# A down projection whose residual is added by an accumulating transfer instead of VectorE

## The chip, the core and the metric

The kernel runs on one core of a Trainium2 chip. The metric is the time of one execution on the device in microseconds (us); the time before is the median of three runs. One profiled execution supplies all the views. TensorE appears in them as PE (matmuls) and PEld (weight loads), VectorE as DVE, ScalarE as ACT, GpSimd as POOL, SyncE as SP.

## What is computed

The reference is a decoder layer of 256 tokens by 2048 channels in float32: gated token mixers, cross-attention into 256 memory tokens, a convolutional gated feed-forward block, and a final RMSNorm. The change touches only the end:

```python
def conv_glu_ffn(u, w_up, conv_w, conv_b, w_down):
    gate, up = jnp.split(u @ w_up, 2, axis=-1)
    gate = causal_dwconv(gate, conv_w, conv_b)
    return (jax.nn.gelu(gate, approximate=False) * up) @ w_down
...
    h = h + conv_glu_ffn(u, ffn_w_up[l], ffn_conv_w[l], ffn_conv_b[l], ffn_w_down[l])
return rms_norm(h, final_norm_g)
```

The down projection is (256 x 5632) times (5632 x 2048). To it the residual `h` is added, each row is scaled by the inverse root of its mean square, and each column by `final_norm_g`.

## The kernel before

Every float32 operand is split into a high and a low part (`hi`, `lo`), and a product is three matmuls: high by high, high by low, low by high. A weight tile of 1 MB (128 x 2048) is loaded by SP into `raw` (three buffers), cast to `hi` by ScalarE and subtracted to `lo` by VectorE (L131 and L132, two pieces of 1024 columns). `hi` and `lo` have five buffers each. `weights()` issues the load and the split of the tile two steps ahead.

**The down projection** runs in two halves of 1024 output columns (`for i in range(2)`). Each half has four output blocks `acc[0..3]` of 128 tokens by 512 columns: blocks 0 and 1 are the first 128 tokens (g = 0), blocks 2 and 3 the others (g = 1). A half is a list of 22 steps over pairs of 128-row slabs of the 5632, and `down_steps` writes the order out by hand:

- an *ordinary step* does two slabs by four blocks by three matmuls: 24 matmuls of 512 columns into `acc`;
- a *seven-product step* (seven per half) does a 2x2 block product by Winograd's scheme with seven block products instead of eight: 21 matmuls. Four of the seven products go to banks of their own, `own[0..3]`, three straight into `acc`. Its weight forms need more preparation (`seven_forms`, L165 to L176): ScalarE casts and VectorE subtracts in turn, and VectorE adds three forms in between. The activation forms come from `input_forms` (L964 to L974), called in the first half alone at `j == 3 * s`.

After the last seven-product step of a half, `own[0..3]` are combined into four blocks `c` (a copy by ScalarE, L1036, and four VectorE operations, L1037 to L1040). The residual comes from `rows_d` in DRAM: four loads of 256 KB into `hr` (two buffers, SP, L1044), each followed by a VectorE addition to `c` (L1045). Two ordinary steps follow in each half while this goes on. In the first half, `acc` is then added to `c` (L1050) and squared for the norm (L1052); the result is kept as `first` and multiplied by `final_norm_g` early in the second half (L995).

**The end of the second half.** The last two steps are held together: block after block gets the 12 matmuls of both, so that block 0 is complete first, and block 3 is done as two pieces of 256 columns. Then, in pinned order, for each block: VectorE adds `acc` to `c` (L1065), ScalarE squares with a row sum (L1067), VectorE multiplies by the norm's weights into `two` (L1069). After block 1 (tokens g = 0) and after the last piece (g = 1): the row sums are reduced (L1073), two small ScalarE operations give the scale `r` (L1074, L1075), VectorE scales the 1024 columns kept from the first half (L1078), ScalarE scales 512 columns of `two` (L1081), VectorE the other 512 (L1083), and three transfers write the rows out. The two halves swap their banks, so `own` of the second half are the `proj` banks, and its `acc` are `lev` (blocks 0 and 1) and `misc` (blocks 2 and 3).

Of the kernel before, what the change touches and what calls it, by code (L numbers as in the profile page):

```python
# [9 lines left out]
F32 = mybir.dt.float32  # L10
# [3 lines left out]
AF = mybir.ActivationFunctionType  # L14
ALU = mybir.AluOpType
# [4 lines left out]
P = 128  # L20
# [29 lines left out]
def down_steps(half):  # L50
    rest = list(range(NST, KF // 2))
    if half:
        rest = rest[-4:] + rest[:-4]
    steps = []
    for s, ordinary in enumerate((3, 2, 2, 2, 2, 1, 1) if half else (2, 2, 2, 2, 2, 2, 1)):
        steps += [(False, rest.pop(0)) for _ in range(ordinary)] + [(True, s)]
    return steps + [(False, k) for k in rest]

# [6 lines left out]
def hybrid_trunk(ctx, tc, xT, memT, par, cst, msk, w_k0, w_ka, w_va, w_hg, w_hv, w_ghg, w_bhg, w_dt,  # L65
                 w_m2, w_gm2, w_bm2, w_out, w_q, w_o, w_up, w_dn, fin_g, outT):
    nc = tc.nc
# [264 lines left out]
    rows_d = dp.tile([T, D], F32, name="rows_d")  # L332
# [651 lines left out]
    for i in range(2):  # L984
        steps = down_steps(i)
        acc = [pj.tile([P, 512], F32, name="proj") for _ in range(4)]
        own = [pl.tile([P, 512], F32, name="lev") for _ in range(2)] \
            + [pm_.tile([P, 512], F32, name="misc") for _ in range(2)]
        if i:
            acc, own = own, acc  # L990
        for j, (seven, q) in enumerate(steps):
            if i == 1 and 4 <= j < 8:

                o = first[:, j - 4, :]
                V.tensor_tensor(out=o, in0=o, in1=gr[:, j % 2 * 512:j % 2 * 512 + 512], op=ALU.mult)  # L995
            if j == 10 * i:
                gr = fd.tile([P, 1024], F32, name="gr")
                nc.sync.dma_start(out=gr, in_=fin_g[i:i + 1, :].partition_broadcast(P))
            last = i == 1 and j >= len(steps) - 2
            if i == 0:  # L1000
                for s in range(NST):
                    if j == 3 * s:
                        input_forms(s)
            w = weights()
            if last and j < len(steps) - 1:
                held = w, q
            elif last:


                for b, c0, c1 in ((0, 0, 512), (1, 0, 512), (2, 0, 512), (3, 0, 256), (3, 256, 512)):  # L1010
                    for x, p in (held, (w, q)):
                        for k in range(2):
                            wh, wl = x(2 * k + b % 2, 512)
                            mm_tok(acc[b][:, c0:c1], inputs(2 * p + k, b // 2),
                                   (wh[:, c0:c1], wl[:, c0:c1]), stop=p == q and k == 1 and c1 == 512)
            elif seven:
                y1, x2, x4 = [(xs[:, q, n, 0:P], xs[:, q, n, P:2 * P]) for n in range(3)]
                a11, y3 = inputs(2 * q, 0), inputs(2 * q, 1)
                a12, a22 = inputs(2 * q + 1, 0), inputs(2 * q + 1, 1)
                one = dict(start=q == 0, stop=q == NST - 1)  # L1020
                mm_tok(own[0], a11, w[0], **one)
                mm_tok(acc[1], x4, w[1])
                mm_tok(own[1], y1, w[2], **one)
                mm_tok(own[2], x2, w[3], **one)
                mm_tok(own[3], y3, w[4], **one)
                mm_tok(acc[0], a12, w[5])
                mm_tok(acc[2], a22, w[6])
            else:
                for k in range(2):
                    for b in range(4):  # L1030
                        mm_tok(acc[b], inputs(2 * q + k, b // 2), w(2 * k + b % 2, 512),
                               start=j == 0 and k == 0, stop=j == len(steps) - 1 and k == 1)
            if seven and q == NST - 1:
                c = fd.tile([P, 4, 512], F32, name="c") if i == 0 else \
                    big.tile([P, 4, 512], F32, name="h")
                S.copy(out=c[:, 0, :], in_=own[0])  # L1036
                V.tensor_tensor(out=c[:, 2, :], in0=own[2], in1=c[:, 0, :], op=ALU.subtract)  # L1037
                V.tensor_tensor(out=c[:, 1, :], in0=own[1], in1=c[:, 2, :], op=ALU.add)
                V.tensor_tensor(out=c[:, 2, :], in0=own[3], in1=c[:, 2, :], op=ALU.add)
                V.tensor_tensor(out=c[:, 3, :], in0=own[1], in1=c[:, 2, :], op=ALU.add)  # L1040
                for b in range(4):
                    hr = fd.tile([P, 512], F32, name="hr", bufs=2)
                    o = 1024 * i + b % 2 * 512
                    nc.sync.dma_start(out=hr, in_=rows_d[b // 2 * P:(b // 2 + 1) * P, o:o + 512])  # L1044
                    V.tensor_tensor(out=c[:, b, :], in0=c[:, b, :], in1=hr,  # L1045
                                    op=ALU.subtract if b == 2 else ALU.add)
        if i == 0:
            for b in range(4):
                g, n = b // 2, b % 2
                V.tensor_tensor(out=c[:, b, :], in0=acc[b], in1=c[:, b, :],  # L1050
                                op=ALU.subtract if b == 2 else ALU.add)
                S.activation(out=acc[b], in_=c[:, b, :], func=AF.Square,  # L1052
                             accum_out=ss[:, g, n:n + 1])
            first = c


    def then(ins):
        tc.keep_in_program_order(ins)

    two = wp.tile([P, 4, 512], F32, name="raw", bufs=3)  # L1060
    for b, c0, c1, slot in ((0, 0, 512, 2), (1, 0, 512, 3), (2, 0, 512, 2), (3, 0, 256, 3),
                            (3, 256, 512, 4)):
        g, n = b // 2, b % 2
        o = c[:, b, c0:c1]
        then(V.tensor_tensor(out=o, in0=acc[b][:, c0:c1], in1=o,  # L1065
                             op=ALU.subtract if b == 2 else ALU.add))
        then(S.activation(out=acc[b][:, c0:c1], in_=o, func=AF.Square,  # L1067
                          accum_out=ss[:, g, slot:slot + 1]))
        then(V.tensor_tensor(out=two[:, b, c0:c1], in0=o, in1=gr[:, n * 512 + c0:n * 512 + c1],  # L1069
# [1 line left out]
        if n == 1 and (g == 0 or slot == 4):  # L1071
            r = fd.tile([P, 2], F32, name="r", bufs=2)
            then(V.tensor_reduce(out=r[:, 0:1], in_=ss[:, g, 0:4 + g], axis=AX.X, op=ALU.add))  # L1073
            then(S.activation(out=r[:, 1:2], in_=r[:, 0:1], func=AF.Ln, bias=eps_t, scale=1.0 / D))  # L1074
            then(S.activation(out=r[:, 1:2], in_=r[:, 1:2], func=AF.Exp, scale=-0.5))  # L1075
            s = r[:, 1:2]
            one = first[:, 2 * g:2 * g + 2, :]
            then(V.tensor_scalar(out=one, in0=one, scalar1=s, scalar2=None, op0=ALU.mult))  # L1078
            nc.sync.dma_start(out=rows[:, g, 0:1024].rearrange("p (n c) -> p n c", n=2), in_=one)
            x, y = two[:, 2 * g, :], two[:, 2 * g + 1, :]  # L1080
            then(S.activation(out=x, in_=x, func=AF.Copy, scale=s))  # L1081
            (nc.scalar if g else nc.sync).dma_start(out=rows[:, g, 1024:1536], in_=x)
            then(V.tensor_scalar(out=y, in0=y, scalar1=s, scalar2=None, op0=ALU.mult))  # L1083
            nc.sync.dma_start(out=rows[:, g, 1536:2048], in_=y)


# [111 lines left out]
```

## Time and profile before

| | |
|---|---|
| median of three runs | 2262.02 us (2260.88 to 2262.89) |
| the profiled execution | 2262.1 us, of which the span of instructions is 2260.3 us |
| PE busy | 2244.1 us, 99% of the span |
| VectorE busy | 1640.1 us, 73% |
| ScalarE busy | 1344.4 us, 59% |
| GpSimd busy | 1.3 us |
| mean granted TensorE clock | 0.998 |

A span is the time from the first instruction to the last. A row of the timeline gives an instruction's start, its duration, its engine and line, what it writes and reads, and in brackets the idle time before it and what ended that. Matmuls are pipelined: one takes 0.39 us from start to end, while the next starts about 0.227 us after it.

### The profile page before, as it was taken

Reading aid. Unit: us, or ns where it says so; the run is one execution under the profiler, and the core shown is the slowest. Engines: PE = TensorE matmul, PEld = TensorE weight load, DVE = VectorE, ACT = ScalarE, POOL = GpSimd, SP = SyncE. Lnnn points to the kernel's source line nnn. Section 1 sums busy time; section 2 is a strip of 40 time slices with the busy share of each in tenths; the row PEclk is TensorE's granted clock in tenths of the full one; section 3 lists DMA queues with packets and bytes.
Section 4 is the critical chain, followed back from the end, with each engine's and each line's share of the span. In section 5 each row is a group of like instructions: output and inputs, shape, how many; then the busy total and the mean of one; then the engine's idle time right before and its main releaser. Section 6 shows DMA issues by size and latency. Waiting matters only on the chain.

```text
span 2260.3 us, 33624 instructions
## 1 busy us (share of the span) xinstructions
PE 2244.1 (99%) x13316; PEld 1937.3 (86%) x13316; DVE 1640.1 (73%) x2648; ACT 1344.4 (59%) x2030; POOL 1.3 (0%) x9
## 2 busy tenths in 40 slices
PE   9999999999999999999999999999999999999997
PEld 8888888888888888888888888888888888888886
DVE  7878879796446677754576755676777777788877
ACT  7566767676446778764456655556555555555544
POOL 0000000000000000000000000000000000000000
PEclk9999999999999999999999999999999999999999
DMA  8744454446555555455566545576555555555653
GB/s 304 247 168 173 167 183 168 168 161 216 193 189 193 179 186 195 168 186 187 194 229 214 202 170 180 177 228 211 190 188 190 193 193 186 186 201 190 233 214 131
DMA packets 86685, 436.91 MB, mean 193 GB/s; under 512 B 24544, under 2 KB 29184, under 8 KB 37504
## 3 DMA queue, kind: packets, MB, share of 16 engines
q1 hardware_dynamic: 69600, 432.36, 54.2%
q10 hardware_dynamic: 16928, 2.42, 0.6%
q8 instruction: 104, 1.70, 0.3%
q14 instruction: 53, 0.43, 0.1%
HBM read 428.42 MB, written 8.42 MB: 193 GB/s over the span
## 4 chain that ended last, share of the span: by engine, by line
PE 96%; DVE 2%; ACT 0%; DMA 0%; issue 0%; DVEq 0%; SPq 0%; ACTq 0%
PE proj L82 88%; PE misc L82 5%; PE lev L82 4%; DVE lo L132 1%; DVE e L523 0%; DVE e L536 0%; DMA raw<-in_w_k 0%; DVE lo L166 0%; PE lev L704 0%; PE lev L768 0%; DMA hr<-rows_d 0%; DVE h L1065 0%; ACT hi L131 0%; PE lev L848 0%; DVE h L1045 0%
## 5 line engine op out<-in xcount | busy, mean ns | idle before, releaser
L132 DVE TENSOR_TENSOR lo<-raw,hi 128x1024 fp32r<-128x1024 f32 x738 | 891.4, 1223 | 438.0 <-ACT hi L131 384.9
L131 ACT CAST hi<-raw 128x1024 fp32r<-128x1024 f32 x737 | 768.1, 1048 | 401.5 <-PE proj L82 387.5
L82 PE MATMUL proj<-s,hi 128*128 128x512 f32 x3952 | 935.0, 392 | 0.6 <-ACT hi L361 0.6
L82 PEld LDWEIGHTS proj<-s,hi 128*128 128x128 f32 x3952 | 732.4, 188 | 146.8 <-ACT hi L131 1.0
L82 PE MATMUL proj<-hi,s 128*128 128x512 f32 x1706 | 534.9, 391 | 0.0
L82 PEld LDWEIGHTS proj<-s,lo 128*128 128x128 f32 x3952 | 495.8, 192 | 12.6 <-ACT s L278 0.5
L82 PE MATMUL proj<-s,lo 128*128 128x256 f32 x3952 | 503.6, 284 | 0.0
L82 PEld LDWEIGHTS proj<-hi,s 128*128 128x128 f32 x1706 | 320.2, 188 | 66.4 <-issue 0.3
L82 PE MATMUL proj<-lo,s 128*128 128x512 f32 x853 | 332.5, 390 | 0.0
L82 PEld LDWEIGHTS proj<-lo,s 128*128 128x128 f32 x853 | 160.2, 188 | 32.2
L263 ACT COPY jt<-proj 128x256 f32<-128x256 f32 x199 | 73.6, 370 | 106.7 <-PE proj L82 106.6
L165 ACT CAST hi<-raw 128x1024 fp32r<-128x1024 f32 (+1 forms) x56 | 51.5, 942 | 89.9 <-DVE raw L173 46.2
L166 DVE TENSOR_TENSOR lo<-raw,hi 128x1024 fp32r<-128x1024 f32 (+1 forms) x56 | 59.9, 1090 | 28.4 <-ACT hi L165 28.0
L667 DVE SCALAR_TENSOR_TENSOR sz<-t,par_t,sz 128x255 f32<-128x255 f32 (+2 forms) x96 | 46.1, 480 | 8.1 <-ACT sz L664 6.9
L935 DVE SCALAR_TENSOR_TENSOR gc<-g,par_t,gc 128x255 f32<-128x255 f32 x88 | 42.3, 480 | 2.0 <-ACT gc L933 0.6
L938 ACT ACTIVATE gc<-gc 128x256 f32<-128x256 f32 x44 | 18.4, 418 | 30.5 <-DVE gc L935 30.5
L82 PE MATMUL proj<-hi,ha 128*128 128x512 f32 x104 | 35.7, 390 | 0.0
L939 DVE TENSOR_TENSOR gc<-gc,r_f 128x256 f32<-128x256 f32 x44 | 18.7, 425 | 21.5 <-ACT gc L938 21.5
L523 DVE TENSOR_TENSOR e<-bb 128x256 f32<-128x256 f32 x96 | 33.6, 420 | 0.0
L536 DVE TENSOR_TENSOR e<-e,kq 128x256 f32<-128x256 f32 x96 | 33.5, 419 | 0.0
L82 PE MATMUL lev<-hi,s 128*128 128x512 f32 x92 | 32.6, 390 | 0.0
L527 ACT ACTIVATE e<-e 128x768 f32<-128x768 f32 x32 | 26.2, 842 | 6.7 <-DVE e L523 6.7
(287 smaller groups left out, 1709.8 us busy)
## 6 DMA issues: line engine op xcount, KB each, us to landing
raw<-in_w_up SPq DMA_DIRECT2D x88, 1024.0 KB, 4.8
raw<-in_w_hg SPq DMA_DIRECT2D x48, 1024.0 KB, 4.8
raw<-in_w_m SPq DMA_DIRECT2D x48, 1024.0 KB, 4.7
raw<-in_w_dn SPq DMA_DIRECT2D x44, 1024.0 KB, 4.8
raw<-in_w_hv SPq DMA_DIRECT2D x16, 1024.0 KB, 4.8
raw<-in_w_ghg SPq DMA_DIRECT2D x16, 1024.0 KB, 4.8
raw<-in_w_bhg SPq DMA_DIRECT2D x16, 1024.0 KB, 4.7
raw<-in_w_gm SPq DMA_DIRECT2D x16, 1024.0 KB, 4.8
```

Source lines behind the costliest of these rows:

```text
L82: ins = PE.matmul(*args, **kwargs)
L131: S.copy(out=hi[:, c - a:d - a], in_=raw[:, c:d])
L132: V.tensor_tensor(out=lo[:, c - a:d - a], in0=raw[:, c:d], in1=hi[:, c - a:d - a].bitcast(F32), op=ALU.subtract)
L165: S.copy(out=hi[:, 0:d - c], in_=raw[:, c:d])
L166: V.tensor_tensor(out=lo[:, 0:d - c], in0=raw[:, c:d], in1=hi[:, 0:d - c].bitcast(F32), op=ALU.subtract)
L263: S.copy(out=tmp, in_=ps[:, T:2 * T])
L523: V.tensor_tensor(out=lev[hw].rearrange("p (n c i) -> p n c i", c=2, i=hw), in0=free(bb, 0, [(2 * hw, nb), (T + hw, 2), (1, hw)]), in1=fre ...
L527: S.activation(out=e[j], in_=e[j], func=AF.Exp)
L536: V.tensor_tensor(out=ev, in0=ev, in1=free(kq, 0, [(2 * hw, nb), (T + hw, 2), (1, hw)]), op=ALU.mult)
L667: V.scalar_tensor_tensor(out=o[:, s:T], in0=raw[:, 0:T - s], scalar=pc("m2_cw", 4 * c + 3 - s), in1=o[:, s:T], op0=ALU.mult, op1=ALU.add)
L935: V.scalar_tensor_tensor(out=gc[:, s:T], in0=g[:, 0:T - s], scalar=pc("f_cw", 3 * c + 2 - s), in1=gc[:, s:T], op0=ALU.mult, op1=ALU.add)
L939: V.tensor_tensor(out=gc, in0=gc, in1=r_f, op=ALU.mult)
```

## The change

Four edits, all in the down projection and the final norm:

1. The residual is added to `c` by one transfer per half with `accum_op=ALU.add`, issued from GpSimd's queue: 128 partitions by two groups of tokens by 1024 columns, 1 MB. The four loads `hr` and the four VectorE additions of a half are gone.
2. The combination of `own` gives block 2 with the other sign, so that all blocks can be added to alike: three `tensor_tensor` and one `scalar_tensor_tensor` instead of four `tensor_tensor`.
3. In both halves an ordinary step moves from before the last seven-product steps to behind them, so that three ordinary steps end a half, not two. The forms of the activations are made at `j == 5 * s // 2`.
4. For tokens g = 0 the scaling is shared in another way: ScalarE takes the 1024 columns of the first half, VectorE the 1024 of `two` in one instruction. For g = 1 nothing but the order in the text changes. The transfers to the output stay.

```diff
-    for s, ordinary in enumerate((3, 2, 2, 2, 2, 1, 1) if half else (2, 2, 2, 2, 2, 2, 1)):
+    for s, ordinary in enumerate((3, 2, 2, 1, 2, 1, 1) if half else (2, 2, 2, 2, 1, 2, 1)):
...
-                    if j == 3 * s:
+                    if j == 5 * s // 2:
                         input_forms(s)
...
                 S.copy(out=c[:, 0, :], in_=own[0])
                 V.tensor_tensor(out=c[:, 2, :], in0=own[2], in1=c[:, 0, :], op=ALU.subtract)
                 V.tensor_tensor(out=c[:, 1, :], in0=own[1], in1=c[:, 2, :], op=ALU.add)
-                V.tensor_tensor(out=c[:, 2, :], in0=own[3], in1=c[:, 2, :], op=ALU.add)
-                V.tensor_tensor(out=c[:, 3, :], in0=own[1], in1=c[:, 2, :], op=ALU.add)
-                for b in range(4):
-                    hr = fd.tile([P, 512], F32, name="hr", bufs=2)
-                    o = 1024 * i + b % 2 * 512
-                    nc.sync.dma_start(out=hr, in_=rows_d[b // 2 * P:(b // 2 + 1) * P, o:o + 512])
-                    V.tensor_tensor(out=c[:, b, :], in0=c[:, b, :], in1=hr,
-                                    op=ALU.subtract if b == 2 else ALU.add)
+                V.tensor_tensor(out=c[:, 3, :], in0=own[3], in1=c[:, 1, :], op=ALU.add)
+                V.scalar_tensor_tensor(out=c[:, 2, :], in0=own[3], scalar=-1.0, in1=c[:, 2, :],
+                                       op0=ALU.mult, op1=ALU.subtract)
+                G.dma_start(out=c.rearrange("p (g n) c -> p g (n c)", g=2),
+                            in_=rows_d.rearrange("(g p) c -> p g c", p=P)[:, :, 1024 * i:1024 * i + 1024],
+                            accum_op=ALU.add)
...
-        then(V.tensor_tensor(out=o, in0=acc[b][:, c0:c1], in1=o,
-                             op=ALU.subtract if b == 2 else ALU.add))
+        then(V.tensor_tensor(out=o, in0=acc[b][:, c0:c1], in1=o, op=ALU.add))
...
-            then(V.tensor_scalar(out=one, in0=one, scalar1=s, scalar2=None, op0=ALU.mult))
+            x, y = two[:, 2 * g, :], two[:, 2 * g + 1, :]
+            if g == 0:
+                then(S.activation(out=one, in_=one, func=AF.Copy, scale=s))
+                then(V.tensor_scalar(out=two[:, 0:2, :], in0=two[:, 0:2, :], scalar1=s, scalar2=None,
+                                     op0=ALU.mult))
+            else:
+                then(V.tensor_scalar(out=one, in0=one, scalar1=s, scalar2=None, op0=ALU.mult))
+                then(S.activation(out=x, in_=x, func=AF.Copy, scale=s))
+                then(V.tensor_scalar(out=y, in0=y, scalar1=s, scalar2=None, op0=ALU.mult))
             nc.sync.dma_start(out=rows[:, g, 0:1024].rearrange("p (n c) -> p n c", n=2), in_=one)
-            x, y = two[:, 2 * g, :], two[:, 2 * g + 1, :]
-            then(S.activation(out=x, in_=x, func=AF.Copy, scale=s))
             (nc.scalar if g else nc.sync).dma_start(out=rows[:, g, 1024:1536], in_=x)
-            then(V.tensor_scalar(out=y, in0=y, scalar1=s, scalar2=None, op0=ALU.mult))
             nc.sync.dma_start(out=rows[:, g, 1536:2048], in_=y)
```

How the instructions stand on VectorE shows two places. The first is the end of the second half, before the change. L132 and L166 are splits of weights, `hr` is the residual's buffer, `h` is the buffer that holds `c`, and the brackets name the semaphores that an instruction waits for (DMAHW: a transfer of SP's or ACT's queue).

```order
L132 TENSOR_TENSOR lo<-raw,hi 128x1024 [waits DMAHW5_49,Activation_49]
L132 TENSOR_TENSOR lo<-raw,hi 128x1024 [waits Activation_49]
L1038 TENSOR_TENSOR h<-proj,h 128x512 [waits DVE_49]
L1045 TENSOR_TENSOR h<-h,hr 128x512
L1039 TENSOR_TENSOR h<-proj,h 128x512 [waits DVE_49]
L1045 TENSOR_TENSOR h<-h,hr 128x512
L1040 TENSOR_TENSOR h<-proj,h 128x512 [waits DVE_49]
L1045 TENSOR_TENSOR h<-h,hr 128x512 [waits DMAHW6_49,DVE_49]
L1045 TENSOR_TENSOR h<-h,hr 128x512 [waits DMAHW7_49]
L1065 TENSOR_TENSOR h<-lev,h 128x512 [waits PE_49]
```

The same place on VectorE after the change, where DMASW1 is the semaphore of the accumulating transfer.

```order
L132 TENSOR_TENSOR lo<-raw,hi 128x1024 [waits DMAHW6_49,Activation_49]
L132 TENSOR_TENSOR lo<-raw,hi 128x1024 [waits Activation_49]
L1039 TENSOR_TENSOR h<-proj,h 128x512 [waits DVE_49]
L1040 TENSOR_TENSOR h<-proj,h 128x512 [waits DVE_49]
L1041 SCALAR_TENSOR_TENSOR h<-proj,h 128x512
L132 TENSOR_TENSOR lo<-raw,hi 128x1024 [waits DMAHW7_49,Activation_49]
L132 TENSOR_TENSOR lo<-raw,hi 128x1024 [waits Activation_49]
L1063 TENSOR_TENSOR h<-lev,h 128x512 [waits DMASW1_49,PE_49]
```

The four additions are gone, the splits of the last step's weights stand behind the combination, and the addition of block 0 waits for the transfer.

The second place is the end of the first half on VectorE, before the change (here `c` is the buffer of that name, `proj` the banks of `acc`).

```order
L1037 TENSOR_TENSOR c<-misc,c 128x512
L132 TENSOR_TENSOR lo<-raw,hi 128x1024 x4
L1038 TENSOR_TENSOR c<-lev,c 128x512
L1045 TENSOR_TENSOR c<-c,hr 128x512
L1039 TENSOR_TENSOR c<-misc,c 128x512
L1045 TENSOR_TENSOR c<-c,hr 128x512
L1040 TENSOR_TENSOR c<-lev,c 128x512
L1194 UNCONDITIONAL_BRANCH
L132 TENSOR_TENSOR lo<-raw,hi 128x1024 x4
L1045 TENSOR_TENSOR c<-c,hr 128x512 x2
L1050 TENSOR_TENSOR c<-proj,c 128x512 x4
```

And after the change:

```order
L1039 TENSOR_TENSOR c<-lev,c 128x512 [waits DVE_49]
L132 TENSOR_TENSOR lo<-raw,hi 128x1024 [waits DMAHW0_49,Activation_49]
L1040 TENSOR_TENSOR c<-misc,c 128x512 [waits DVE_49]
L1041 SCALAR_TENSOR_TENSOR c<-misc,c 128x512
L132 TENSOR_TENSOR lo<-raw,hi 128x1024 [waits Activation_49]
L132 TENSOR_TENSOR lo<-raw,hi 128x1024 [waits DMAHW1_49,Activation_49]
L132 TENSOR_TENSOR lo<-raw,hi 128x1024 [waits Activation_49]
L1196 UNCONDITIONAL_BRANCH
L132 TENSOR_TENSOR lo<-raw,hi 128x1024 [waits DMAHW2_49,Activation_sequencer_49,PE_49]
L1049 TENSOR_TENSOR c<-proj,c 128x512 [waits DMASW0_49,PE_49]
L132 TENSOR_TENSOR lo<-raw,hi 128x1024 [waits Activation_49]
```

Four splits of weights now stand between the finished combination (L1041) and the first instruction that waits for the transfer (L1049), and one split, the second piece of the second half's second step, stands right behind that instruction.

More of the change, by code (lines that the diff above doesn't have):

```diff
@@ L1049, in hybrid_trunk @@
                 g, n = b // 2, b % 2
-                V.tensor_tensor(out=c[:, b, :], in0=acc[b], in1=c[:, b, :],
-                                op=ALU.subtract if b == 2 else ALU.add)
+                V.tensor_tensor(out=c[:, b, :], in0=acc[b], in1=c[:, b, :], op=ALU.add)
                 S.activation(out=acc[b], in_=c[:, b, :], func=AF.Square,
```

## The prediction

> **What bounds the kernel now.** I read the page first, then the busy time by stretches, then the chain of waits over the last microseconds, then the timelines of VectorE and PE there.
>
> ```profile
> span 2260.3 us, 33624 instructions
> PE 2244.1 (99%) x13316; PEld 1937.3 (86%) x13316; DVE 1640.1 (73%) x2648; ACT 1344.4 (59%) x2030; POOL 1.3 (0%) x9
> PE 96%; DVE 2%; ACT 0%; DMA 0%; issue 0%; DVEq 0%; SPq 0%; ACTq 0%
> ```
>
> PE sets the time: 96% of the chain that ended last. The profiled execution took 2262.1 us, its span 2260.3; the median of the runs is 2262.02, so a saving in the span is taken off the median as it stands. About 0.2%, or 4.5 us, is what a measurement of this kernel can tell from no change.
>
> The busy time by stretches covers the down projection (start and length, then busy time of PE, PEld, DVE, ACT):
>
> ```profile
> 2010.00:2130.00 120.00, 120.00 (x538) 99.58 (x537) 104.47 (x150) 63.61 (x79) 0.00 (x0) 1.00 0.57 207
> 2130.00:2230.00 100.00, 100.00 (x441) 82.56 (x441) 79.23 (x86) 49.85 (x59) 0.00 (x0) 1.00 0.56 209
> 2230.00:2247.00 17.00, 16.86 (x83) 13.47 (x82) 14.58 (x18) 6.64 (x9) 0.00 (x0) 1.00 0.12 31
> 2247.00:2260.00 13.00, 0.00 (x0) 0.00 (x0) 6.96 (x15) 5.09 (x16) 0.00 (x0) 0.59 0.41 161
> ```
>
> Up to 2230 PE never stands still, whatever the others do. So everything that the change takes from VectorE, ScalarE or the queues before that is worth nothing by itself. PE's work is the same before and after (same number of steps of each kind). Only the last 13 us, in which PE is idle, can get shorter. The chain of waits there:
>
> ```profile
> 2242.02 3.09 DMA hr<-rows_d
> 2245.11 0.02 issue
> 2245.14 0.69 DVE h L1045
> 2245.83 0.61 DVE h L1065
> ...
> 2249.30 0.75 DVE c L1078
> 2250.05 0.39 DVE raw L1083
> 2250.45 0.61 DVE h L1065
> ...
> 2254.44 0.75 DVE c L1078
> 2255.19 0.40 DVEq L1194
> ```
>
> And from the timelines, the last matmul of PE, VectorE's addition of block 0 and its addition of the last piece:
>
> ```profile
> 2246.65 0.28 PE L82 MATMUL misc<-hi,s 128*128 128x256 f32 x1
> 2245.75 0.68 DVE L1065 TENSOR_TENSOR h<-lev,h 128x512 f32<-128x512 f32 x1
> 2252.68 0.42 DVE L1065 TENSOR_TENSOR h<-misc,h 128x256 f32<-128x256 f32 x1
> ```
>
> PE has finished everything at 2246.93. Yet the last piece is added at 2252.68, 5.75 us later, because VectorE starts on block 0 only at 2245.75: it waits for the third and fourth residual load, whose buffers came free late. From there VectorE and ScalarE work through a fixed row of operations to the end, 2260.3 - 2245.75 = 14.55 us. The end is thus set by the moment at which `c`, residual included, is complete.
>
> **The change part by part.** *Step order.* The pace of PE, and where the last seven-product step begins, before:
>
> ```profile
> 2118.63 12.26 PE proj L82 x54
> 2230.27 0.39 PE L82 MATMUL proj<-hi,ha 128*128 128x512 f32 x1
> 2234.96 4.63 DVE L132 TENSOR_TENSOR lo<-raw,hi 128x1024 fp32r<-128x1024 f32 x4 [0.26 <-ACT hi L131]
> 2239.51 0.68 DVE L1038 TENSOR_TENSOR h<-proj,h 128x512 f32<-128x512 f32 x1
> 2240.11 0.68 DVE L1045 TENSOR_TENSOR h<-h,hr 128x512 f32<-128x512 f32 x1
> ```
>
> 54 matmuls in 12.26 us are 0.227 us each: an ordinary step is 24 of them, 5.45 us, a seven-product step 21, 4.77 us. With one ordinary step more behind it, the last seven-product step starts 5.45 us earlier, at 2224.8, and the steps ahead of it (ordinary, seven, ordinary, seven) are the same as before, so VectorE's splits shift along. The four L132 then end at 2234.1 and the next combination, at 2239.51 before, starts at 2234.06. Three combinations follow at VectorE's pitch of 0.60 us; the last is a `scalar_tensor_tensor`, bounded by 0.68 us (L1038's row) and twice the 0.48 us of the nearest row with half the columns:
>
> ```profile
> L667 DVE SCALAR_TENSOR_TENSOR sz<-t,par_t,sz 128x255 f32<-128x255 f32 (+2 forms) x96 | 46.1, 480 | 8.1 <-ACT sz L664 6.9
> ```
>
> So `c` without residual is ready at 2236.0 (2236.2 at most). The two L132 of the last step (half of the four's 4.63 us) come behind it, at 2236.0 to 2238.3; PE wants them from 2237.0 on. Some tenths of waiting there replace the waits of PE's weight loads of the last 40 us before:
>
> ```profile
> PEld lev L82 <- DVE lo L132: 0.5, 1, 0.5
> PEld misc L82 <- DVE lo L166: 0.4, 1, 0.4
> ```
>
> So I leave PE's end at 2246.9.
>
> *The transfer.* No GpSimd transfer and no accumulation is in the trace. The nearest rows are those of the last 40 us, when a transfer has the queues to itself, and the one over all `hr` loads (times are from issue to landing):
>
> ```profile
> raw<-in_w_dn SPq DMA_DIRECT2D x2, 1024.0 KB, 4.7
> hr<-rows_d SPq DMA_DIRECT2D x2, 256.0 KB, 3.1
> DMA to landing us min/median/max: 3.1/4.6/4.9
> ```
>
> 256 KB alone take 3.1 us, 1 MB alone 4.7: so 2.1 us for each MB on top of 2.6. The lower bound of the accumulating transfer is the plain 4.7. It has to read 1 MB from DRAM and 1 MB of `c` to write 1 MB; if only the moving part doubles, it takes 2.6 + 4.3 = 6.9 us, if all of it does, 9.4. The upper bound is four pieces of 256 KB one after the other at 4.6 each, 18.4. I take 8.2, the middle of 6.9 and 9.4, since no row prices the issue from GpSimd's queue either. The Trainium skill ("Collectives: The Full Stack", section on the bandwidth ceiling) says that an add inside a transfer costs nothing by itself but needs two source reads, which halves the rate; no run so far shows it here. The same skill's "DMA: Bandwidth & Descriptors" (anatomy of one DMA on the GpSimd path) fits 2.0 us plus bytes over 436 GB/s, which would be an estimate of 4.4 us for 1 MB, and by it the sum would be the whole 5.75 us.
>
> *The tail.* For g = 0 VectorE has one instruction of 1024 columns (0.75 us, as L1078) where it had two; L1083's 0.39 us leaves the chain. ScalarE's scaling of 1024 columns lies beside it: by L1081's row it would be at most twice 0.72 us, from 2249.30 to 2250.74 in the old times, and the next square, pulled forward, starts at 2251.08 - 0.39 = 2250.69. That hides it.
>
> ```profile
> 2249.30 0.72 ACT L1081 ACTIVATE raw<-raw,r 128x512 f32<-128x512 f32 x1
> 2251.08 0.60 ACT L1067 ACTIVATE misc<-h 128x512 f32<-128x512 f32 x1 [1.06 <-DVE h L1065]
> ```
>
> *The sum.* From the addition of block 0 to the end there are 14.55 - 0.39 = 14.16 us. The transfer lands at 2236.0 + 8.2 = 2244.2, the span ends at 2258.4, and 1.9 us are saved: 2262.0 - 1.9 = 2260.1. In general the saving is 10.1 us less the transfer's time. It cannot pass 5.75 us, since the last piece cannot be added before PE ends; that is reached at a transfer of 4.4 us.
>
> *The first half.* VectorE, before, at the same place, and PE at the seam of the halves:
>
> ```profile
> 2117.99 0.69 DVE L1037 TENSOR_TENSOR c<-misc,c 128x512 f32<-128x512 f32 x1
> 2118.59 4.62 DVE L132 TENSOR_TENSOR lo<-raw,hi 128x1024 fp32r<-128x1024 f32 x4
> ...
> 2130.89 1.36 PE lev L82 x6
> ```
>
> 5.45 us earlier, the four L132 end at 2117.8; three combinations and one L132 later `c` is ready, at about 2121. L1049 behind it is not wanted before PE ends the half at 2130.9, and queued behind L1049 is the split that PE needs at 2130.9 + 5.45 + 2.72 = 2139.1. With 0.6 us for L1049 and 1.2 for the split the transfer may take 16 us at no cost, weight loads beside it included. Cost: nothing. Without the `hr` loads SP's weight loads come earlier, and as PE never waits there, that too is worth nothing.
>
> *Splits in the new order.* Where seven, ordinary and seven follow each other, VectorE needs more time than PE; with two ordinary steps between, less. The first L166 of neighbouring seven-product steps:
>
> ```profile
> 2081.82 1.23 DVE L166 TENSOR_TENSOR lo<-raw,hi 128x1024 fp32r<-128x1024 f32 x1 [1.09 <-ACT hi L165]
> 2097.04 1.23 DVE L166 TENSOR_TENSOR lo<-raw,hi 128x1024 fp32r<-128x1024 f32 x1 [1.17 <-ACT hi L165]
> ...
> 2213.92 1.22 DVE L166 TENSOR_TENSOR lo<-raw,hi 128x1024 fp32r<-128x1024 f32 x1
> ...
> 2225.59 1.22 DVE L166 TENSOR_TENSOR lo<-raw,hi 128x1024 fp32r<-128x1024 f32 x1
> ```
>
> 11.67 us against PE's 10.22 lose 1.45; 15.22 against 15.67 win 0.45 at the least. The change adds one such single pair in each half, but two ordinary steps follow it, and in the first half the `input_forms` are done by then in VectorE's order. Cost taken: nothing.
>
> **The rivals.** *A plain price* (0.20): the adding costs the transfer nothing, and it lands like the last weight loads, 4.7 us after issue. For it: those rows, and the idle queues. Against: it reads twice. At 2236.0 + 4.7 = 2240.7 the end is 2254.9: 5.4 us saved, 2256.6.
>
> *The transfer comes late* (0.12): the addition of block 0 waits longer for the transfer than before for `hr`, with all that is pinned behind it on VectorE and ScalarE. It decides from 10.1 us on, and is visible as slower from 14.6 on. For it: one transfer must be whole before block 0 can begin, where the four loads let two blocks go ahead; 18.4 us gives an end of 2236.0 + 18.4 + 14.16 = 2268.6, 8.3 us slower, 2270.3. Against: the engines move 1 MB alone in 4.7.
>
> *PE starves at the new single pairs* (0.08): if the 1.45 us isn't won back before the last seven-product step, PE ends 1.5 to 2.9 us later, and with it the sum, 2261.6 to 2263.0. For it: PE's two waits above stand right behind two such pairs in a row. Against: they are 0.9 us together.
>
> **How the numbers follow.** The forecast, a transfer of 5.6 to 14.6 us, has 0.60, the three rivals 0.20, 0.12 and 0.08. The third mostly stays within 0.2%: 0.06 of it. So faster by over 0.2% 0.20, within 0.2% 0.66, slower 0.14. The range: below, the full 5.75 us and 0.5 us of PE's waits, 2255.8; above, a transfer of 15 us, 4.9 us slower, 2267.0.
>
> **What would show it.** Right: the addition of block 0 (L1063) begins at about 2244 and ends a wait for the transfer; GpSimd issues it at 2236; PE ends near 2246.9; L1077 never delays a square. Wrong: a transfer of under 5.6 or over 14.6 us; PE ending later than 2247.5; a wait of PE at the seam of the halves; or block 0 waiting for PE alone, which would leave the saving at 5.75.

## The result, and the profile after

The changed kernel takes 2270.28 us (median of six runs, 2269.99 to 2270.76), the kernel before 2261.98 in the same comparison: a ratio of 1.0038 (1.0025 to 1.0051), slower by 0.38%. The forecast was 2260.1, with a range that ended at 2267.0.

The profiled execution of the kernel after took 2270.3 us. From its page:

```profile
span 2268.5 us, 33620 instructions
PE 2247.5 (99%) x13316; PEld 1937.1 (85%) x13316; DVE 1633.7 (72%) x2639; ACT 1344.6 (59%) x2030; POOL 3.8 (0%) x11
```

The span is 8.2 us longer. PE has the same 13316 matmuls and is 3.4 us longer busy, which no edit asks for. Where the end is made, VectorE's timeline after (start, length, and in brackets the wait before):

```profile
2243.89 0.68 DVE L1041 SCALAR_TENSOR_TENSOR h<-proj,h 128x512 f32<-128x512 f32 x1
2244.49 2.35 DVE L132 TENSOR_TENSOR lo<-raw,hi 128x1024 fp32r<-128x1024 f32 x2
2254.31 0.69 DVE L1063 TENSOR_TENSOR h<-lev,h 128x512 f32<-128x512 f32 x1 [7.47 <-DMA h<-rows_d]
```

and PE's last matmul and the end of the chain of waits:

```profile
2255.10 0.28 PE L82 MATMUL misc<-hi,s 128*128 128x256 f32 x1
```

```profile
2245.09 9.12 DMA h<-rows_d
...
2262.61 0.75 DVE c L1081
2263.36 0.40 DVEq L1196
```

The picture of the end is the one forecast: VectorE finishes `c` (L1041), the splits follow, block 0 waits for the transfer, and 2268.5 - 2254.31 = 14.19 us later all is over (forecast 14.16). But all of it stands 8 us too late. `c` without residual is ready at 2244.57, not at 2236.0, and PE ends at 2255.38, 8.45 us later than before. The time went before the end, at the seam of the halves. PE's busy time there, by stretches (start and end, length, busy time and matmuls, granted clock, DMA share, GB/s):

```profile
2130.00:2136.00 6.00, 6.00 (x28) 1.00 0.82 227
2136.00:2140.00 4.00, 0.81 (x3) 0.96 0.00 0
2140.00:2145.00 5.00, 4.63 (x11) 0.50 0.37 115
2145.00:2150.00 5.00, 5.00 (x21) 0.85 0.56 192
2150.00:2155.00 5.00, 5.00 (x24) 1.00 0.55 218
```

First PE stands still for 3.2 of 4 us; then it works at half the granted clock, 11 matmuls in 5 us where later 24 fit. The timelines of GpSimd, ScalarE, VectorE and PE show who held it:

```profile
2121.62 1.33 POOL L1043 DMA_DIRECT2D c<-rows_d  x1 [2016.36 <-ACT hi L131]
```

```profile
2136.55 1.28 ACT L128 ACT_TABLE_LOAD   x1 [12.74 <-PE misc L82]
```

```profile
2139.09 1.23 DVE L132 TENSOR_TENSOR lo<-raw,hi 128x1024 fp32r<-128x1024 f32 x1 [14.03 <-ACTq L127]
```

```profile
2139.05 0.50 PE L82 MATMUL lev<-hi,h 128*128 128x512 f32 x1 [2.74 <-ACTq L127]
2140.37 0.80 PE L82 MATMUL lev<-lo,h 128*128 128x512 f32 x1 [0.81 <-DVE lo L132]
```

ScalarE waits 12.74 us before a table load (L127 and L128: the functions that the norm needs at the end, loaded beside the second tile of the second half). Behind it, on ScalarE, stands the split of that tile, then VectorE's part of the split, then PE. The transfer's landing, from the DMA issues of that stretch and of the last one (median us from issue to landing):

```profile
c<-rows_d POOLq DMA_DIRECT2D x1, 1024.0 KB, 14.4
...
h<-rows_d POOLq DMA_DIRECT2D x1, 1024.0 KB, 9.1
```

2121.62 + 14.4 = 2136.0: the table load starts half a microsecond after the transfer has landed. The releaser that the row names, a matmul that ended at 2136.3, is not what held it. What the load really waits for stands in the order of ScalarE's instructions after the change: it is written as a critical section, a stretch of the program whose start waits here for every queue and engine with earlier work, and DMASW0 is the semaphore of the accumulating transfer.

```
L1196 UNCONDITIONAL_BRANCH [waits DMAHW1_49,DMAHW2_49,DMAHW0_49,DMAHW3_49,DMASW0_49,DMAHW4_49,Activation_sequencer_49,DMAHW5_49,DVE_49,DMAHW6_49,PE_49,DMAHW7_49,Activation_49,Pool_49]
L128 ACT_TABLE_LOAD
```

These waits are seven instructions of ScalarE's sequencer. In nanoseconds (shortest, median, longest) they took:

```profile
L1196 ACTq EVENT_SEMAPHORE  x7: 17/38/8228, 2125.6 to 2136.3; - x7
```

The long one is the wait for DMAHW3 and DMASW0, from 2127.81 to 2136.04; DMAHW3, a weight load, had landed at 2127.79. But DMASW0 is not alone in being late. DMAHW4, next in the list, is a weight load that was issued at 2125.09, beside the transfer. It took 10.6 us, where the load of the same tile in the kernel with the new order and the four plain loads (the first experiment below, issued at 2125.92, and there not waited for by the section) took 5.5:

```profile
raw<-in_w_dn SPq DMA_DIRECT2D x1, 1024.0 KB, 10.6
raw<-in_w_dn SPq DMA_DIRECT2D x1, 1024.0 KB, 5.5
```

It landed at 2135.7, 0.3 us before the transfer. So the transfer holds the section twice over, by its own landing and by that of the weight load, and with DMASW0 off the list the load would have started at most 0.3 us sooner (an estimate from these two landings).

The kernel before has the same section without DMASW0, and its timeline of ScalarE showed a small wait of the same kind. The row names the residual, but the waits in the section's own list ended with a weight load, issued at 2123.24, that landed at 2128.35:

```profile
2128.77 1.28 ACT L128 ACT_TABLE_LOAD   x1 [3.91 <-DMA hr<-rows_d]
```

### The profile page after: what moved, and what is told of

The parts are those of the page before. It is cut to its first block, busy times and chain, and to the rows that moved or that the text cites. A ratio compares the mean times of both kernels' runs of the same rounds, so it can differ in the third digit from the quotient of the medians.

```text
span 2268.5 us, 33620 instructions
## 1 busy us (share of the span) xinstructions
PE 2247.5 (99%) x13316; PEld 1937.1 (85%) x13316; DVE 1633.7 (72%) x2639; ACT 1344.6 (59%) x2030; POOL 3.8 (0%) x11
## 5 line engine op out<-in xcount | busy, mean ns | idle before, releaser
L132 DVE TENSOR_TENSOR lo<-raw,hi 128x1024 fp32r<-128x1024 f32 x738 | 891.0, 1221 | 449.4 <-ACT hi L131 385.6
L166 DVE TENSOR_TENSOR lo<-raw,hi 128x1024 fp32r<-128x1024 f32 (+1 forms) x56 | 59.9, 1088 | 25.4 <-ACT hi L165 25.2
L938 ACT ACTIVATE gc<-gc 128x256 f32<-128x256 f32 x44 | 18.4, 418 | 30.5 <-DVE gc L935 30.5
```

The lines of the kernel that those rows point to most:

```text
L132: V.tensor_tensor(out=lo[:, c - a:d - a], in0=raw[:, c:d], in1=hi[:, c - a:d - a].bitcast(F32), op=ALU.subtract)
L166: V.tensor_tensor(out=lo[:, 0:d - c], in0=raw[:, c:d], in1=hi[:, 0:d - c].bitcast(F32), op=ALU.subtract)
```

## The experiments

Theory A: the transfers are the whole loss, the first by holding the table load at the seam, the second by taking 9.6 us from the ready `c` to its landing; the new order of the steps is worth something. Theory D: at the seam not the table load alone, but also the additions of `acc` (L1049) that stand on VectorE in order hold the splits. Rivals B (the order of the steps starves PE) and C (the second transfer is the loss) were tried first.

**The steps alone.** The kernel before, with edit 3 only:

```diff
-    for s, ordinary in enumerate((3, 2, 2, 2, 2, 1, 1) if half else (2, 2, 2, 2, 2, 2, 1)):
+    for s, ordinary in enumerate((3, 2, 2, 1, 2, 1, 1) if half else (2, 2, 2, 2, 1, 2, 1)):
-                    if j == 3 * s:
+                    if j == 5 * s // 2:
```

> The kernel before with the new step order and the new times of the activation forms alone; the residual still by four loads and VectorE. Theory A (the loss is the scalar engine's table load at the seam of the halves, which waits for the accumulating transfer): no transfer, no stall at the seam, PE ends within 3 us of before (2247 to 2250) and block 0 is added some 4 us earlier; about 2257 to 2260 us. Rival B (the new order starves PE): PE ends at about 2255 as in the changed kernel; 2266 us or more.

2258.77 us (2257.68 to 2260.96), ratio 0.9988 (0.998 to 0.9997). PE loses nothing at the seam. It ends at 2248.07, 1.1 us later than before, after three waits for VectorE's splits (0.51 us at 2115.01, 0.26 at 2220.32, 0.22 at 2230.48) that the kernel before doesn't have. The table load, and the addition of block 0:

```profile
2128.99 1.28 ACT L128 ACT_TABLE_LOAD   x1 [4.62 <-PE proj L82]
```

```profile
2242.29 0.69 DVE L1065 TENSOR_TENSOR h<-lev,h 128x512 f32<-128x512 f32 x1 [0.28 <-PE lev L82]
```

The order alone wins about 3 us, and block 0 no longer waits for the residual but for PE. B falls. Four plain loads bring the residual in time, so there was nothing left for a transfer to win at the end.

**The transfer in the second half alone.** The kernel after, with the four loads and additions back in the first half:

```diff
-                G.dma_start(out=c..., in_=rows_d..., accum_op=ALU.add)
+                if i == 1:
+                    G.dma_start(out=c..., in_=rows_d..., accum_op=ALU.add)
+                else:
+                    for b in range(4):
+                        ...  # hr load and addition, as before
```

> The changed kernel with the accumulating transfer in the second half alone; the first half has the four loads and VectorE's additions again. Theory A: the table load waits no more for the transfer, PE ends at about 2247, the transfer of the second half takes 9 us as in the changed kernel, and block 0 begins at about 2245.6: 2261 to 2262 us, the same as before. Rival B (step order): 2268 us or more. Rival C (the second transfer is the loss, as the prediction's rival had it): 2268 us or more with PE ending at 2247.

2262.42 us (2261.79 to 2264.9), ratio 1.0004 (0.9995 to 1.0013). That is 0.4 us above A's range. There is no loss at the seam; the transfer takes 8.9 us and block 0 waits for it:

```profile
2247.36 0.69 DVE L1070 TENSOR_TENSOR h<-lev,h 128x512 f32<-128x512 f32 x1 [7.23 <-DMA h<-rows_d]
```

So the second transfer costs 3.7 us against the steps alone, and 7.9 us of the kernel after's time hang on the first. C falls.

**The transfer in the first half alone, in the old order.**

```diff
-    for s, ordinary in enumerate((3, 2, 2, 1, 2, 1, 1) if half else (2, 2, 2, 2, 1, 2, 1)):
+    for s, ordinary in enumerate((3, 2, 2, 2, 2, 1, 1) if half else (2, 2, 2, 2, 2, 2, 1)):
...
-                    if j == 5 * s // 2:
+                    if j == 3 * s:
...
+                if i == 0:
                     G.dma_start(out=c..., in_=rows_d..., accum_op=ALU.add)
+                else:
+                    ...  # hr loads and additions, as before
```

> The old step order with the accumulating transfer in the first half alone; the second half has the four loads. Theory A: the combination is ready 5.4 us later than in the changed kernel, the transfer lands that much later, and the stall at the seam grows from about 8 us to about 13: 2273 to 2277 us. Rival B (step order): no loss, 2261 to 2263 us. Rival C: no loss either.

2267.61 us (2266.89 to 2270.11), ratio 1.0026 (1.0015 to 1.0037). Slower, but by less than expected, and not through the table load. In the old order the transfer is issued behind the table load's section, whose list does not hold it. It takes 12.8 us and lands at 2139.0; the addition of the first half's products waits for it, and PE loses 1.9 us and 2.1 us behind that:

```profile
2139.13 2.48 DVE L1056 TENSOR_TENSOR c<-proj,c 128x512 f32<-128x512 f32 x4 [5.86 <-DMA c<-rows_d]
```

```profile
2140.00:2150.00 10.00, 8.09 (x35) 1.00 0.37 127
2150.00:2170.00 20.00, 17.86 (x75) 1.00 0.45 173
```

That speaks for D: there is a second way from the transfer to PE.

**The table load earlier.** The kernel after, with the load eight tiles earlier:

```diff
-        last = state["issued"] == len(order) - KF // 2 + 2
+        last = state["issued"] == len(order) - KF // 2 - 6
```

> The changed kernel with the scalar engine's table load moved from the split of the second half's second tile to the split of a tile in the first half (step 15 of it), ahead of the transfer; both transfers stay. Theory A: no stall at the seam though the first transfer still takes about 14 us; PE ends at 2247 to 2248, about 2261 to 2262 us. Rival B: 2268 us or more. Rival D (it is not the table load but the additions of the first half, which wait for the transfer too): PE still stalls at the seam, by some 5 us or more: 2267 us or more.

2270.77 us (2269.95 to 2271.45), ratio 1.0041 (1.0028 to 1.0053): A's number was missed by 9 us. The section waits at its new place too, and PE loses 1.9 us there:

```profile
2091.78 1.28 ACT L128 ACT_TABLE_LOAD   x1 [4.07 <-PE proj L82]
```

```profile
2090.00:2110.00 20.00, 18.08 (x76) 1.00 0.47 171
...
2150.00:2170.00 20.00, 17.81 (x75) 1.00 0.59 227
```

With all that later, the transfer is issued at 2126.20, lands at 2140.98, and the addition L1049 waits for it for 8.6 us, with the splits behind it: 2.2 us of PE between 2150 and 2170. D's time (2267 us or more) is met, but not its stall of 5 us at the seam. The row of L1049 names a matmul as its releaser; the chain of waits names the transfer.

```profile
2141.07 0.69 DVE L1049 TENSOR_TENSOR c<-proj,c 128x512 f32<-128x512 f32 x1 [8.63 <-PE misc L82]
```

```profile
2126.20 14.78 DMA c<-rows_d
```

**The table load later**, seven tiles behind its place, and so behind the addition:

```diff
-        last = state["issued"] == len(order) - KF // 2 + 2
+        last = state["issued"] == len(order) - KF // 2 + 9
```

> The kernel after, with ScalarE's table load moved seven tiles later in the second half, behind the addition of the first half's products: the accumulating transfer has landed long before it. Theory A (at the seam it is the table load that waits for the transfer, and with it the splits of the second half's second tile and TensorE): the 3.5 us of idle TensorE at 2136 to 2140 and the half clock behind it go; the additions of the first half's products wait for the transfer up to 2136 us instead and hold the splits behind them on VectorE by some 3 us, of which TensorE may lose 0 to 3; the table load costs up to 3 at its new place: 2261 to 2267 us. Theory D (the in-order additions hold VectorE just as the table load did): the loss moves and does not shrink, 2268 to 2271 us.

2271.0 us (2269.96 to 2271.84), ratio 1.004 (1.0027 to 1.0052): D's number. The clock stays at 1.00 and the stall at 2136 is gone, but L1049 now waits for the transfer in plain sight, and the section costs more at its new place:

```profile
2137.48 0.69 DVE L1049 TENSOR_TENSOR c<-proj,c 128x512 f32<-128x512 f32 x1 [8.84 <-DMA c<-rows_d]
```

```profile
2140.00:2150.00 10.00, 9.41 (x42) 1.00 0.73 251
2150.00:2170.00 20.00, 18.19 (x76) 1.00 0.43 164
2170.00:2220.00 50.00, 47.31 (x202) 1.00 0.51 188
```

Of PE's idle time 2.4 us lie behind the addition (0.6 and 1.8) and 2.7 behind the section at its new place, so D's number was met in part for another reason. The two waits stand one behind the other; taking one away bares the other. What has to go is the late landing itself.

**Why does it land so late?** Two kernels write the residual over `c` instead of adding it, once from GpSimd's queue and once from SyncE's. In both the `own` products are thereby left out of the result.

```diff
                 G.dma_start(out=c..., in_=rows_d...,
-                            accum_op=ALU.add)
+                            )
```

> The kernel after, with the same two 1 MB transfers from GpSimd's queue, but writing the residual over the combinations and not adding to them (the 'own' products are left out of the sum). Theory A (the adding itself is what takes 9.1 and 14.4 us): the second half's transfer takes 4 to 6 us and the first half's 5 to 9 us, the table load behind it starts by 2131, TensorE loses nothing or under 2 us at the seam, and the time is 2256 to 2260 us. Rival Q (GpSimd's queue, or one transfer of 1 MB in place of four of 256 KB, is what is slow, and the adding is free): 9 and 14 us stay, the clock falls to 0.50 behind the stall, and the time stays at 2269 to 2271 us. In between, if adding is only part of it.

```diff
-                G.dma_start(out=c..., in_=rows_d..., accum_op=ALU.add)
+                nc.sync.dma_start(out=c..., in_=rows_d...)
```

> As the run before (the residual is written over the combinations, so that the 'own' products are left out), but issued by SyncE, in whose queue the weight loads stand. Theory A (adding sets the transfer's time): 4 to 6 us in the second half, 5 to 9 in the first; but the weight loads behind the transfer on SyncE are not issued until the combinations are ready, so up to 3 us may be lost to weights that come late: 2256 to 2262 us. Rival Q (GpSimd's queue is slow): this kernel is at 2256 to 2260 us while the run before stays near 2270 us.

2264.95 us (2263.63 to 2266.36), ratio 1.0014 (1.0005 to 1.0023), from GpSimd; 2259.89 us (2259.19 to 2262.29), ratio 0.9992 (0.9983 to 1.0), from SyncE. The landings from GpSimd's queue, first and second half, and the table load:

```profile
c<-rows_d POOLq DMA_DIRECT2D x1, 1024.0 KB, 9.6
...
h<-rows_d POOLq DMA_DIRECT2D x1, 1024.0 KB, 6.0
```

```profile
2134.63 1.28 ACT L128 ACT_TABLE_LOAD   x1 [10.56 <-DMA raw<-in_w_dn]
```

and from SyncE's:

```profile
c<-rows_d SPq DMA_DIRECT2D x1, 1024.0 KB, 5.9
...
h<-rows_d SPq DMA_DIRECT2D x1, 1024.0 KB, 5.5
```

```profile
2130.49 1.28 ACT L128 ACT_TABLE_LOAD   x1 [6.06 <-PE proj L82]
```

So neither A nor Q was the whole of it. Adding makes the transfer half as long again: 6.0 to 9.1 us by itself, 9.6 to 14.4 us beside the weight loads; it is worth 2270.28 - 2264.95 = 5.3 us of the kernel. GpSimd's queue is near SyncE's by itself (6.0 against 5.5) but far behind beside weight loads (9.6 against 5.9); that is worth 5.1 us. Why the queue matters there is not settled: that GpSimd's transfer gets a smaller share beside SyncE's was not tried apart from the weight loads' own delay. In the GpSimd row above the table load waits for a weight load, although the transfer had landed by about 2131.4: issued at 2125.35, beside the transfer, that load took 8.8 us and landed at 2134.1.

**The residual early.** All of the change but the transfer: one plain transfer from SyncE fills free columns of the buffer of the input forms ahead of time, and VectorE adds.

```diff
+            if j == 4:
+                nc.sync.dma_start(out=hr..., in_=rows_d...)
...
-                G.dma_start(out=c..., in_=rows_d..., accum_op=ALU.add)
+                for b in range(4):
+                    V.tensor_tensor(out=c[:, b, :], in0=c[:, b, :], in1=hr[:, b // 2, b % 2, :], op=ALU.add)
```

> The order, the combinations and the shared scaling of the kernel after, but the residual of each half is loaded by one plain transfer from SyncE into a free part of the buffer of the input forms, ten or more steps before it is needed, and VectorE adds it in four 128x512 additions. Theory A (the order is worth its gain, the transfer alone is the loss): no stall at the seam; no wait of VectorE for the residual in the second half; TensorE ends at 2247 to 2248, and the time is 2256 to 2259 us, at or under the 2258.8 of the steps alone. Rival (the residual's arrival was not what held the end in the steps alone): 2258 to 2259, no gain on it.

2261.36 us (2260.8 to 2262.59), ratio 0.9998 (0.9989 to 1.0007), a miss of both. VectorE never waits for the residual, but the scheduler had put the second half's transfer at the seam, ahead of a weight load. The transfer itself (2121.68 to 2127.4) was not what the section waited for in the end: it was that weight load, which took 7.1 us beside it and landed at 2131.06. PE loses 1.5 us:

```profile
2131.47 1.28 ACT L128 ACT_TABLE_LOAD   x1 [8.04 <-DMA raw<-in_w_dn]
```

```profile
2140.00:2150.00 10.00, 9.24 (x41) 1.00 0.53 202
2150.00:2170.00 20.00, 19.26 (x84) 1.00 0.47 178
```

**The same, with the second transfer pinned to the middle of the second half**, and, in a further kernel, **the steps alone with the shared scaling** (edits 3 and 4, residual as before).

```diff
-            if j == 4:
+            if j == (14 if i else 4):
+                ...  # pinned among the weight loads
```

> The kernel before this (residual early, by one plain transfer from SyncE into free columns), with the second half's transfer moved from the seam to the middle of the second half. Theory A (whatever transfer stands ahead of the table load delays it, since the load waits for all that were issued before; that cost the kernel with the early residual 1.5 us of TensorE at the seam): the table load starts by 2129.5 and TensorE loses under 0.5 us between 2136 and 2170; VectorE waits in the second half for TensorE and not for the residual, the last stretch is as in the steps alone less 0.4: 2257.8 to 2259.5 us. Rival (the seam's loss there had another reason): table load at 2131 to 2132 again, 2261 us.

> The kernel before with the new order of the steps and the shared scaling of the first tokens, and the residual as before, by four loads from SyncE in each half. Theory A (the transfers are the whole loss): no stall at the seam, the sum of the two parts: 2258.8 of the steps alone less 0.4, so 2257.8 to 2259 us. Rival (the order and the sharing do not add up, or the chip used for the steps alone was a fast one): 2259.5 to 2262 us.

2259.39 us (2258.5 to 2261.46), ratio 0.9991 (0.9982 to 1.0), for the first, and 2259.66 us (2257.2 to 2261.28), ratio 0.9992 (0.9983 to 1.0001), for the second. In the first, as Theory A expected, the table load is back at its time, and block 0 waits for PE:

```profile
2128.99 1.28 ACT L128 ACT_TABLE_LOAD   x1 [5.71 <-PE proj L82]
```

```profile
2242.65 0.69 DVE L1071 TENSOR_TENSOR h<-lev,h 128x512 f32<-128x512 f32 x1 [0.93 <-PE lev L82]
```

In the second, the steps' gain and the scaling's 0.4 us did not show as a sum: it lies 0.9 us above the steps alone, within the scatter of both, and in the range of the rival (the parts do not add up, or the steps alone ran on a faster chip), which stays open. The steps alone and these two, 2258.8 to 2259.7, lie 2 to 3 us below the kernel before; the upper ends of their ratios, 0.9997, 1.0 and 1.0001, say that this gain is barely told from none. The steps alone are the simplest and the lowest.

Over the kernels with the new order and the table load in its old place, the last landing that the section waits for, the start of that load and what PE loses between 2136 and 2170 go together. In all but the last row it is a weight load that lands last:

| kernel | last landing | table load at | PE idle, 2136 to 2170 |
|---|---|---|---|
| steps and scaling | 2127.9 | 2128.18 | 0 us |
| steps alone | 2128.7 | 2128.99 | 0 |
| residual in the middle | 2128.5 | 2128.99 | 0 |
| second half only | 2129.6 | 2129.81 | 0 |
| plain, SyncE | 2130.0 | 2130.49 | 0.2 |
| residual early | 2131.1 | 2131.47 | 1.5 |
| plain, GpSimd | 2134.1 | 2134.63 | 3.2 |
| after | 2136.0 (the transfer; a weight load at 2135.7) | 2136.55 | 3.6, and half clock |

## Why the prediction was wrong

**The step that failed is "the first half": "the transfer may take 16 us at no cost … Cost: nothing".** It asked who waits for the transfer on VectorE and found L1049. It did not ask who else does. ScalarE's table load waits for all transfers issued ahead of it, and is late from about 2130.5 on (table above), 9 us after `c` was ready, not 16. Nor did it ask what the transfer does to the others: it took the weight loads to come earlier, and one of them landed at 2135.7, where the same tile's landed at 2131.5 in the steps alone. Two signs were passed over: the wait for a transfer at L128 in the trace of before, and, in the order after the change, the split ahead of L1049 that waits for ScalarE's sequencer. Even on VectorE 16 us was too much: with the table load out of the way the transfer landed 2137.4, 15.5 us after `c` was ready, and PE still lost 2.4 us (0.6 and 1.8 in the rows of the late table load). And 14.4 us beside weight loads is near the end of that margin; the sum's 8.2 us held for neither half.

What that step cost: between VectorE's first combination (L1038 after, L1037 in the steps alone) in the first half and in the second lie 2236.24 - 2112.57 = 123.67 us after, 2228.91 - 2113.14 = 115.77 in the steps alone: 7.9 us. Of them 3.55 are PE's two waits (2.74 and 0.81). The chain of waits after gives what follows, in rows of five or six matmuls that take 1.14 to 1.36 us at the full pace:

```profile
2140.37 2.50 PE lev L82 x5
2142.87 2.56 PE misc L82 x6
2145.43 1.91 PE lev L82 x6
2147.35 1.36 PE misc L82 x6
```

(2.50 - 1.14) + (2.56 - 1.36) + (1.91 - 1.36) = 3.1 us lost to the clock. Where the rest, 1.2 us, went stays open.

**The transfer in the second half**: right in its mechanism, mis-sized in its term. From the ready `c` to the addition of block 0 it is 2254.31 - 2244.57 = 9.74 us, not 8.2: 0.5 to the issue, 9.1 to the landing. The price of the adding lies between the plain 4.7 and the upper bound of 9.4 for doubling all, near the upper one. So the saving of 1.9 us would have been 0.36.

**The sum**, with what was measured: 2258.4 forecast for the span, 8.6 for the late `c`, 1.5 for the transfer, 0.0 for the tail: 2268.5. Not all of the 8.6 is the seam's: the steps alone, without a loss there, come to the first combination of the second half at 2228.91, where the forecast's shift gives 2233.26 - 5.45 = 2227.81, so 1.1 us are the new order's.

**The splits in the new order, and PE's end**: put at nothing, but they cost about 1 us. In the steps alone PE waits 0.99 us for splits in the three places above and ends at 2248.07, beyond the 2247.5 that the prediction gave as a sign of being wrong. That is the mechanism of the rival "PE starves", below its 1.5 to 2.9 us. **The tail**: right, 14.19 us; ScalarE's scaling of 1024 columns took 1.15 us and delayed nothing. **The cap of 5.75 us** by a fast transfer was too high: with the residual in time, block 0 starts at 2242.65, waiting for PE, and not at 2240.7. The span of that kernel is 2256.7 us: not 5.4 but 3.6 us were to be won, by the two profiled executions; by the medians it is 2.3.

**The rivals.** "The transfer comes late" gave 2270.3 and the result is 2270.28, but that is chance: it put the delay into the second half, with 18.4 us of transfer, and the second half took 9.6. The right rival, a wait at the seam, stood in the prediction's last part as a sign of failure and had neither a price nor a chance. The plain price was worked out as if from SyncE: there it is 5.5 us, from GpSimd 6.0, and with the adding 9.1.

## What to carry to other kernels

A new transfer has more waiters than the instruction that uses its data: look on every engine for barriers and critical sections behind its issue in the program, and read their wait lists, since the trace's releaser names one instruction only, and here more than once the wrong one. It also slows the transfers beside it, and these have waiters of their own. When several things queue behind one late arrival, moving one of them away bares the next; bring the arrival forward. Before an accumulating transfer is put in place of plain loads and an idle engine's additions, try the rest of the change without it: here what gain there was came with the reordering.

## What the runs showed of the hardware

- An accumulating transfer of 1 MB took 9.1 us by itself and 14.4 beside weight loads, a plain one from the same queue 6.0 and 9.6, from SyncE's 5.5 and 5.9. A weight load of 1 MB issued 3.5 us behind it took 10.6 us beside the accumulating one and 8.8 beside the plain one from GpSimd's queue; the load of the same tile took 5.5 in the steps alone. The Trainium skill ("Collectives: The Full Stack", section on the bandwidth ceiling) would have the adding halve the rate by its second read; here the whole time grew by half.
- After waits of 2.74 and 0.81 us with one matmul between them, PE ran at a granted clock of 0.50, at a pace of 0.43 us a matmul, for some 6 us. The clock's own record has the half from 2139.65, inside the second wait, to 2146.48, 6.83 us. In the kernels whose idle time at the seam came in shorter pieces (0.57 and 0.81 us in the plain transfer from GpSimd, at most 1.58 in the transfer in the old order) the clock stayed at 1.00. The Trainium skill ("TensorE: Matmul & The Clock Gate", Part 1) gives an idle window of about 3.4 us that halves the clock and as long a busy one that restores it, and has the windows run free of the kernel. The half agrees. The clock fell after less idle time than such a window (2.74 us and 0.1 of the second wait), and it came back after two of them, 6.83 us. Most of the second wait lies in the first of the two; whether that is the reason is not shown.
